# Experts ordered by token count on the chip, with 128, 64 or 32 slots each

## The chip, the cores and the metric

The kernel runs on one core of a Trainium2 chip. The metric is the device time of one launch in microseconds. Before the change three runs took 777.27, 777.66 and 778.37 us; the median is 777.66.

## The reference

One layer of a hybrid diffusion block on 256 context tokens and 256 latent tokens with 1024 channels, all in fp32:

```
mod  = SiLU(c) @ w_ada                      # shift, scale, gate; context and latent have their own c
h    = rms_norm(x) * (1 + scale) + shift
p    = h @ w_in                             # split among four mixers: SSD, GLA, RG-LRU, attention
x    = x + gate * (merge(mixers(p)) @ w_out)
h    = rms_norm(x) * (1 + scale2) + shift2  # latent tokens only from here
group  = top-1 of 4 groups; experts = top-2 of the 4 experts in that group; weights by softmax
out  = x + gate2 * sum over the two experts of  w * (silu(h @ w1[e]) * (h @ w3[e])) @ w2[e]
```

There are 16 experts with 512 inner channels; w1, w3 and w2 of one expert are 6 MB in fp32, so all experts together are 96 MB. Each latent token goes to two experts, 512 pairs in all.

## The kernel before, in words

**Front.** `ada` (L956 to L969) multiplies the two conditioning vectors with the modulation weights. The vectors stand in four columns of the array, two for the value rounded to fp32r and two for what the rounding leaves (`cs4`). A 1 MB load of weights comes as two halves; the even one is used in fp32 (L965), the odd one is split by ACT into a rounded part `whi` (L865) and by DVE into the rest `wlo` (L866), and both are multiplied (L968). `hk(k)` (L971 to L986) turns the sums of a channel block into columns (L975), transposes the normalized tokens (L979) and applies shift and scale.

**Middle.** The projection into the mixers, the mixers and the output projection run from L885 to L1812. The diff doesn't touch them.

**Routing.** The logits give one-hot marks `M` of the two experts of each token. A matmul with a triangle of ones counts, for each token and expert, the tokens ahead of it (`prv`), and a matmul of ones the tokens per expert. `val` (L388) is each token's slot in its expert, `cnt` (L393) the counts. `xh` and `xo` (L376) are the normalized tokens as rounded value and rest. `places` (L402 to L442) finds the first expert of 4 to 15 with over 64 tokens and exchanges it with position 11.

**Experts.** Each position has 64 slots, position 11 has 128 (`TWICE`). PE's order is written by hand. `one_hot` (L452) compares slots with a row of numbers and gives a matrix S of tokens by slots; `gather` (L481) multiplies tokens with S for four positions at once (256 columns), each of eight channel blocks with value and rest, and DVE scales the result (L487). `slot_weights` (L470) gives the routing weight of each slot. For an expert, `s1` (L506) computes w1 and w3 with 64 columns of the array each: w1 on the upper half HI, w3 on the lower half LO, 512 output columns each. `s1p` (L513, L514) does SiLU and product, `pick` (L521) transposes S, `s2` (L529) transposes the activations, `s3` (L542) multiplies with w2, two halves of the output on two halves of the array. ey, eyh and eyl (L549 to L551) scale with the gate and split into value and rest, `s4` (L557) scatters them with S back to tokens, adding into the two PSUM sums `eo0` and `eo1` over all experts. At the end eight additions (L658) and two transfers write the output.

Written order for each expert e: first half of s1(e+1), pick(e), s4(e-1), s2(e), second half of s1(e+1), s3(e). After every fourth expert the gather of the next four positions is spread around s3.

**Loads.** The 96 loads of 1 MB are issued by SP in the order of use into 15 buffers; a load waits until PE has read the buffer's former content. **Overflow.** At the very end a loop runs once per block of slots that no position had room for; with no such block it runs zero times.

Of the kernel before, what the change touches and what calls it, by code (L numbers as in the profile page):

```python
# [191 lines left out]
NE = 16  # L192
# [5 lines left out]
TWICE = 11  # L198
# [3 lines left out]
class Moe:  # L202


    def __init__(self, tc, I, xl, ident, identb, kp):
# [9 lines left out]
        self.identb = identb  # L215
        self.eps = kp.tile([128, 1], F32, name="eps2")
# [18 lines left out]
        self.ohu = kp.tile([128, NE], U8, name="ohu")  # L235
# [3 lines left out]
        self.val = kp.tile([128, 3, NE], F32, name="val")  # L239
        self.vp = kp.tile([128, 3, NE], F32, name="vp")  # L240
        self.Wp = kp.tile([128, 2, NE], F32, name="Wp")
        self.oh = kp.tile([128, NE], F32, name="oh")
        self.dif = kp.tile([128, 3, NE], F32, name="dif")
        self.ids = kp.tile([128, NE], mybir.dt.int32, name="ids")
        G.iota(self.val[:, 2], pattern=[[1, NE]], base=0, channel_multiplier=0, allow_small_or_imprecise_dtypes=True)
        self.prio = kp.tile([128, 2, NE], F32, name="prio")
        G.iota(self.prio[:, 0], pattern=[[-1, NE]], base=NE, channel_multiplier=0, allow_small_or_imprecise_dtypes=True)
        G.memset(self.prio[:, 0, 0:FIXED], 0.0)
        G.memset(self.prio[:, 1], 0.0)
        G.memset(self.prio[:, 1, TWICE:TWICE + 1], 0.5)  # L250
        self.cnt = kp.tile([128, NE], F32, name="cnt")
# [90 lines left out]
    def route(self, tp, tb):  # L342
# [22 lines left out]
        V.tensor_copy(self.ogt, self.og)  # L365
# [33 lines left out]
    def places(self):  # L399
# [3 lines left out]
        L, mg, og, le, ml, ex, rg = self.L, self.mg, self.og, self.le, self.ml, self.ex, self.rg  # L403
        M, W = self.M, self.W
        b4 = lambda ap: ap[:, :, None].to_broadcast([128, 2, 4])
        oh, m, ohu = self.oh, self.mo[:, 0:1], self.ohu
        vp, val = self.vp, self.val
        V.scalar_tensor_tensor(oh, self.cnt, float(CAP), self.prio[:, 0], op0=OP.is_gt, op1=OP.mult)
        V.tensor_tensor(oh, oh, self.prio[:, 1], op=OP.max)
        V.reduce_max(m, oh, axis=AX.X)  # L410
        V.tensor_copy(vp, val)
        V.tensor_scalar(ohu, oh, m, None, op0=OP.is_equal)
        P = slice(TWICE, TWICE + 1)
        V.copy_predicated(vp, ohu[:, None, :].to_broadcast([128, 3, NE]), val[:, :, P].to_broadcast([128, 3, NE]))
        V.tensor_scalar(oh, oh, m, None, op0=OP.is_equal)
        V.tensor_mul(self.dif, val, oh[:, None, :].to_broadcast([128, 3, NE]))
        V.reduce_sum(vp[:, :, P], self.dif, axis=AX.X)
# [20 lines left out]
        d = self.dif[:, 0:2]  # L438
        V.tensor_copy(self.Wp, self.W)
        V.copy_predicated(self.Wp, ohu[:, None, :].to_broadcast([128, 2, NE]), self.W[:, :, P].to_broadcast([128, 2, NE]))  # L440
        V.tensor_mul(d, self.W, oh[:, None, :].to_broadcast([128, 2, NE]))
        V.reduce_sum(self.Wp[:, :, P], d, axis=AX.X)  # L442

    def slots(self, g):

        self.S64 = self.kp.tile([128, 2, GE, CAP], F32R, name="S64", bufs=1)
        for t in range(2):
            i = self.one_hot(self.S64[:, t], (self.vp if g else self.val)[:, t, g * GE:g * GE + GE], GE)
        return i
# [6 lines left out]
    def run(self, out, mp, rp, ps, dump):  # L456
# [9 lines left out]
        def slot_weights(dst, n, Sx, Wx, c=CAP):  # L466
            p = tb()
            for i in range(n):
                for t in range(2):
                    T.matmul(p[0:c, i:i + 1], Sx(t, i).bitcast(F32), Wx(t, i), start=t == 0, stop=t == 1)  # L470
            V.tensor_copy(dst, p[0:c, 0:n])
# [18 lines left out]
        class Block:  # L490
            def __init__(self):
                self.wide, self.cs = False, [slice(0, 512)]
# [3 lines left out]
        def s1(b, half, post=True):  # L496
# [13 lines left out]
        def s1p(b):  # L510
            n = 2 * CAP if b.wide else CAP
            b.a = mp.tile([128, 512], F32, name="ef", bufs=2)[0:n]
            b.last = S.activation(b.a, b.p[0] if b.wide else b.p[0][HI], AF.Silu)  # L513
            b.last2 = V.scalar_tensor_tensor(b.a, b.a, b.w, b.p[1][0:n], op0=OP.mult, op1=OP.mult)  # L514

        def pick(b):
            n = 2 * CAP if b.wide else CAP
# [7 lines left out]
        def s2(b):  # L525
            n = 2 * CAP if b.wide else CAP
            ptv = tb()[:, 0:4 * n].rearrange("p (k s) -> p k s", k=4)
            for k in range(4):
                T.transpose(ptv[:, k], b.a[:, k * 128:k * 128 + 128], ident[0:n, 0:n])  # L529
            b.at = mp.tile([128, 4, 128], F32, name="eat", bufs=2)[:, :, 0:n]  # L530
            S.copy(b.at, ptv)

        def s3(b):
            n = 2 * CAP if b.wide else CAP
            p = (tb(), tb()) if b.wide else (tb(),) * 2
            for i in range(2):
                r = b.load(4 + i)
                for j in range(2):
                    k = 2 * i + j
                    for hf, pr in enumerate((slice(0, n), slice(0, n) if b.wide else HI)):  # L540
# [3 lines left out]
            for hf in range(2 if b.wide else 1):  # L544
# [3 lines left out]
                for s in b.cs:  # L548
                    V.tensor_mul(q[:, s], p[hf][:, s], self.gw[:, hf, s] if b.wide else self.gp[:, s])  # L549
# [4 lines left out]
        def s4(b):  # L554
            for s, i, t in [(s, i, t) for s in b.cs for i in range(2) for t in range(2)]:
                for hf, pr in enumerate((slice(0, 128),) * 2 if b.wide else (LO, HI)):
                    T.matmul(b.f[hf][:, t, s], b.st[pr, t], b.y[hf if b.wide else 0][i][pr, s],  # L557
                             start=b.start and i == 0, stop=b.stop and i == 1 and s is b.cs[-1])

        f = [ps.tile([128, 2, 512], F32, name=f"eo{hf}", bufs=1) for hf in range(2)]  # L560
        xgs = {}
        order = tc.manual_schedule(engines={mybir.EngineType.PE})
        order.__enter__()

# [5 lines left out]
        with tc.issue_after(group(0, at=4).ins):  # L570
            self.places()

        def expert(e):
# [7 lines left out]
            b.load, b.f, b.start, b.stop = load, f, e == 0, e == NE - 1  # L581
            if e == NE - 1:
                b.cs = [slice(0, 256), slice(256, 512)]
# [3 lines left out]
            b.x = lambda k: xgs[e // GE][:, k, (e % GE) * CAP:(e % GE) * CAP + CAP]  # L587
            b.Sb = lambda t: S64b[e // GE][:, t, e % GE]
# [14 lines left out]
        def weights(g):  # L603
            S64 = self.S64
            slot_weights(ws[:, g * GE:g * GE + GE], GE, lambda t, e: S64[:, t, e],
                         lambda t, e: Wp[:, t, g * GE + e:g * GE + e + 1])
            S64b[g] = kp.tile([128, 2, GE, CAP], BF, name="S64b", bufs=2)
# [10 lines left out]
        for hf, pr in enumerate((LO, HI)):  # L618
            V.tensor_copy(self.gp[pr], self.gw[pr, hf])
        for e in range(NE):  # L620
# [3 lines left out]
            if e % GE == GE - 2 and e < NE - GE:  # L624
                self.slots(e // GE + 1)
                weights(e // GE + 1)
# [7 lines left out]
            if e % GE == GE - 1:  # L634
# [19 lines left out]
        def add_out(f):  # L654
            for c, t in ((0, 0), (0, 1), (1, 0), (1, 1)):
                for hf in range(2):
                    s = slice(hf * 512 + c * 256, hf * 512 + c * 256 + 256)
                    V.tensor_add(xl[:, t, s], xl[:, t, s], f[hf][:, t, c * 256:c * 256 + 256])  # L658
# [1205 lines left out]
```

## Time and profile before

| | |
|---|---|
| median of three runs | 777.66 us |
| profiled execution: its own time | 779.12 us |
| span of that execution | 777.4 us |
| mean granted TensorE clock | 0.981 |
| PE busy | 747.6 us, 96% |
| DVE busy | 454.2 us, 58% |
| ACT busy | 394.4 us, 51% |
| bytes moved | 186.59 MB, mean 240 GB/s |

The profiled execution is one launch recorded by the hardware; its span runs from the first instruction to the last. A busy PE is not PE at its best rate: matmuls are pipelined and the records of neighbours overlap. The granted clock is a share of 2.4 GHz; 0.50 is 1.2 GHz.

### The profile page before, as it was taken

Reading aid. Unit: us, or ns where it says so; the run is one execution under the profiler, and the core shown is the slowest. Engines: PE = TensorE matmul, PEld = TensorE weight load, DVE = VectorE, ACT = ScalarE, POOL = GpSimd, SP = SyncE. Lnnn points to the kernel's source line nnn. Section 1 sums busy time; section 2 is a strip of 40 time slices with the busy share of each in tenths; the row PEclk is TensorE's granted clock in tenths of the full one; section 3 lists DMA queues with packets and bytes.
Section 4 is the critical chain, followed back from the end, with each engine's and each line's share of the span. In section 5 each row is a group of like instructions: output and inputs, shape, how many; then the busy total and the mean of one; then the engine's idle time right before and its main releaser. Section 6 shows DMA issues by size and latency. Waiting matters only on the chain.

```text
span 777.4 us, 10064 instructions
## 1 busy us (share of the span) xinstructions
PE 747.6 (96%) x3702; PEld 494.4 (64%) x3702; DVE 454.2 (58%) x875; ACT 394.4 (51%) x650; POOL 16.9 (2%) x74
## 2 busy tenths in 40 slices
PE   7999999997999999999999999998999999999994
PEld 3267787875888877767878788885444354444442
DVE  3576786986883699889687866645112122203223
ACT  6468669899945697566456544533212121212111
POOL 3000000000000000000000001000000000000000
PEclk9999999999899999999999999998999999999998
DMA  8764221223444255446645698738999999999921
GB/s 332 284 228 173 111 67 69 109 61 120 138 159 140 106 193 207 150 158 231 220 144 190 222 357 310 306 140 330 416 426 427 424 427 424 427 427 406 392 91 56
DMA packets 29043, 186.59 MB, mean 240 GB/s; under 512 B 3312, under 2 KB 3472, under 8 KB 9152
## 3 DMA queue, kind: packets, MB, share of 16 engines
q1 hardware_dynamic: 27760, 182.03, 60.4%
q0 software_dynamic: 1088, 3.37, 1.6%
q8 instruction: 30, 0.49, 0.2%
q10 hardware_dynamic: 144, 0.52, 0.2%
q14 instruction: 21, 0.17, 0.1%
HBM read 184.87 MB, written 1.05 MB: 239 GB/s over the span
## 4 chain that ended last, share of the span: by engine, by line
PE 77%; DVE 9%; ACT 7%; DMA 4%; issue 2%; SPq 0%; DVEq 0%; ACTq 0%
PE eh L506 16%; PE mm L885 12%; PE mm L886 11%; PE mm L887 11%; PE etp L542 8%; PE eo L557 2%; DMA lr<-in_adar_dram 2%; DMA xl<-in_x_dram 2%; DVE wlo L866 1%; ACT L785 1%; PE tp L1118 1%; PE mm L965 1%; PE eh L481 1%; ACT whi L865 1%; PE etp L481 1%
## 5 line engine op out<-in xcount | busy, mean ns | idle before, releaser
L865 ACT CAST whi<-raw 128x1024 fp32r<-128x1024 f32 x109 | 114.3, 1049 | 100.7 <-PE mm L887 70.6
L866 DVE TENSOR_TENSOR wlo<-raw,whi 128x1024 fp32r<-128x1024 f32 x109 | 132.7, 1219 | 55.1 <-ACT whi L865 54.2
L506 PE MATMUL eh<-eraw,xg 128*64 128x512 f32 x480 | 108.9, 596 | 0.3 <-DVE xg L487 0.3
L886 PE MATMUL mm<-wlo,hhi 128*128 128x512 f32 x240 | 98.6, 411 | 1.6 <-DVE wlo L866 1.6
L885 PE MATMUL mm<-whi,hhi 128*128 128x512 f32 x240 | 97.9, 411 | 0.0
L887 PE MATMUL mm<-whi,hlo 128*128 128x512 f32 x240 | 96.2, 402 | 0.0
L506 PEld LDWEIGHTS eh<-eraw,xg 128*64 128x64 f32 x480 | 34.6, 137 | 57.8 <-issue 52.6
L514 DVE SCALAR_TENSOR_TENSOR ef<-ef,wslot,eh 64x512 f32<-64x512 f32 x15 | 11.1, 739 | 99.1 <-ACT ef L513 99.1
L885 PE MATMUL mm<-hhi,whi 128*128 128x512 f32 (+1 forms) x168 | 67.0, 399 | 0.0
L886 PE MATMUL mm<-hlo,whi 128*128 128x512 f32 (+1 forms) x168 | 66.4, 395 | 0.0
L887 PE MATMUL mm<-hhi,wlo 128*128 128x512 f32 (+1 forms) x168 | 65.3, 389 | 0.0
L542 PE MATMUL etp<-eraw,eat 128*64 128x512 f32 (+1 forms) x256 | 61.4, 594 | 1.4 <-DVE xg L487 0.8
L885 PEld LDWEIGHTS mm<-whi,hhi 128*128 128x128 f32 x240 | 45.5, 190 | 13.0 <-issue 3.3
L886 PEld LDWEIGHTS mm<-wlo,hhi 128*128 128x128 f32 x240 | 45.7, 190 | 12.1 <-DVE wlo L866 1.9
L887 PEld LDWEIGHTS mm<-whi,hlo 128*128 128x128 f32 x240 | 45.6, 190 | 11.3 <-issue 1.1
L785 ACT ACT_TABLE_LOAD x39 | 50.0, 1283 | 0.8
L1085 DVE SCALAR_TENSOR_TENSOR lr<-lr,la 128x1024 f32<-128x1024 f32 x32 | 39.0, 1220 | 11.8 <-DMA lr<-in_adar_dram 11.6
L542 PEld LDWEIGHTS etp<-eraw,eat 128*64 128x64 f32 (+1 forms) x256 | 19.9, 140 | 38.2 <-issue 35.1
L513 ACT ACTIVATE ef<-eh 64x512 f32<-64x512 f32 (+1 forms) x16 | 9.5, 594 | 60.6 <-PE eh L506 60.6
L550 ACT CAST eyh<-ey 128x512 fp32r<-128x512 f32 (+1 forms) x18 | 10.6, 595 | 52.8 <-DVE ey L549 45.3
L887 PEld LDWEIGHTS mm<-hhi,wlo 128*128 128x128 f32 x168 | 31.6, 188 | 8.1 <-issue 1.5
L885 PEld LDWEIGHTS mm<-hhi,whi 128*128 128x128 f32 x168 | 31.6, 188 | 7.7 <-DVE lr L1085 0.8
(487 smaller groups left out, 1231.5 us busy)
## 6 DMA issues: line engine op xcount, KB each, us to landing
eraw<-in_ew_dram SPq DMA_DIRECT2D x96, 1024.0 KB, 12.4
raw<-in_ws_dram SPq DMA_DIRECT2D x59, 1024.0 KB, 4.8
lr<-in_adar_dram SPq DMA_DIRECT2D x32, 512.0 KB, 3.4
xc<-in_ctx_dram SPq DMA_DIRECT2D x1, 1024.0 KB, 7.1
xl<-in_x_dram SPq DMA_DIRECT2D x1, 1024.0 KB, 13.0
lw<-in_lw_dram POOLq DMA_DIRECT2D x4, 256.0 KB, 3.0
xl<-in_x_dram POOLq DMA_DIRECT2D x1, 1024.0 KB, 6.2
out_dram<-xl SPq DMA_DIRECT2D x1, 512.0 KB, 2.8
```

What stands on the lines that cost most here:

```text
L481: T.matmul(q, x[:, t, k * 128:k * 128 + 128], Sx(t), start=j == 0 and t == 0, stop=j == 1 and t == 1)
L506: T.matmul(b.p[m][pr], b.x(k), r[:, c:c + 512], start=k == 0, stop=k == 7)
L514: b.last2 = V.scalar_tensor_tensor(b.a, b.a, b.w, b.p[1][0:n], op0=OP.mult, op1=OP.mult)
L542: T.matmul(p[hf][pr], b.at[:, k], r[:, c:c + 512], start=k == 0, stop=k == 3)
L557: T.matmul(b.f[hf][:, t, s], b.st[pr, t], b.y[hf if b.wide else 0][i][pr, s], start=b.start and i == 0, stop=b.stop and i == 1 and s is b. ...
L785: S.activation(o, i, func, **kw)
L865: S.copy(hi, r)
L866: V.tensor_sub(lo, r, hi.bitcast(F32))
L885: T.matmul(ps, l[0], r[0], start=start, stop=False)
L886: T.matmul(ps, l[0], r[1], start=False, stop=False)
L887: lastmm[0] = T.matmul(ps, l[1], r[0], start=False, stop=stop)
L1085: V.scalar_tensor_tensor(r, r, 1.0, cb, op0=OP.mult, op1=OP.mult, accum_out=lcol[:, j, k:k + 1])
```

## The change

Experts 4 to 15 are ranked on the chip by their token counts, with 12 x 12 comparisons on DVE, and slots, identities and routing weights are moved to the ranked positions with products and sums (`move`). Position 9 gets the largest (128 slots), positions 4 to 8 the next five (64 slots), positions 10 to 15 the six smallest (32 slots, `FEW`). Experts 0 to 3 keep their positions. There are three gathers instead of four: positions 0 to 3, 4 to 7, and 8 with 10 to 15 (64 + 6 x 32 = 256 slots).

A position with 32 slots uses four quarters of the array's columns: w1 and w3 have two quarters each, with 256 output columns a quarter, and so has w2. Its s2 has two transposes instead of four, its scatter four row quarters of 256 columns. The sums `eo` are four PSUM tiles of 256 columns by two token blocks; they are zeroed once by matmuls with a zero matrix, and every scatter adds to them. A 64-slot scatter has 16 programs of 256 columns instead of 8 of 512. The last expert's predecessor has its scatter half before and half behind the last w2. Counts are copied by ACT right behind `val`. The overflow table has 15 entries of two numbers instead of 7.

In the front, `ada` uses all weights in fp32, without the split, as 32 programs on four column quarters (`cz` holds the two vectors and 30 zero columns; the quarters are summed afterwards by `pk`). Behind every four programs stand eight programs on the identity matrix whose result isn't used (`warm`). `hm` forms the modulation of four channel blocks at once.

The core of the diff:

```diff
-TWICE = 11
+TWICE = 9
+FEW, HALF = 10, 32
+GROUPS = [[(0, 4, CAP)], [(4, 4, CAP)], [(8, 1, CAP), (FEW, 6, HALF)]]
...
         V.scalar_tensor_tensor(self.val[:, 0:2], M, -1000.0, prv[:, 0:2], op0=OP.mult, op1=OP.add)
+        S.copy(self.cnt, prv[:, 2])
         self.last = i = self.slots(0)
         for t, h in ((1, 0), (0, 1), (1, 1)):
             i = low(t, h, i)
+        self.low = i
         with tc.issue_after(i.ins):
-            V.tensor_copy(self.cnt, prv[:, 2])
+            V.tensor_copy(self.ogt, self.og)
...
+        V.scalar_tensor_tensor(key, self.cnt[:, FIXED:NE], float(NE), self.kio, op0=OP.mult, op1=OP.add)
+        V.tensor_tensor(self.sq, row(key), down(key), op=OP.is_gt)
+        V.reduce_sum(rk, self.sq, axis=AX.X)
+        V.tensor_tensor(self.pm, row(rk), down(self.want), op=OP.is_equal)
+        def move(dst, src, n):
+            V.tensor_mul(self.dif[:, 0:n], src[:, :, None, FIXED:NE].to_broadcast([128, n, NS, NS]),
+                         self.pm[:, None].to_broadcast([128, n, NS, NS]))
+            V.reduce_sum(dst[:, :, FIXED:NE], self.dif[:, 0:n], axis=AX.X)
+            V.tensor_copy(dst[:, :, 0:FIXED], src[:, :, 0:FIXED])
...
+                    if b.few:
+                        for q in range(4):
+                            c = (2 * j + 1 - q // 2) * 512 + q % 2 * 256
+                            T.matmul(b.p[0][q * 32:q * 32 + 32, 0:256], b.x(k), r[:, c:c + 256], start=k == 0, stop=k == 7)
+                        continue
...
+                    if b.few:
+                        for q in range(4):
+                            T.matmul(p[0][q * 32:q * 32 + 32, 0:256], b.at[:, k % 2, k // 2 * 32:k // 2 * 32 + 32],
+                                     r[:, j * 1024 + q * 256:j * 1024 + q * 256 + 256], start=k == 0, stop=k == 3)
+                        continue
...
+                if b.few:
+                    for q in range(4):
+                        r = slice(q * 32, q * 32 + 32)
+                        T.matmul(b.f[q][:, t], b.st[r, t], b.y[0][i][r, 0:256], start=False, stop=b.stop and i == t == 1)
+                    continue
...
+            for p in f:
+                T.matmul(p.rearrange("p t (a b) -> p (t a) b", a=2), self.zero,
+                         identb[:, None, :].to_broadcast([128, 4, 128]), start=True, stop=False)
...
+                s4(B[e - 1], (0,))
                 s3(B[e])
-                s4(B[e - 1])
+                s4(B[e - 1], (1,))
                 s4(B[e])
...
-        NB, NF = 7, 3 * NE
+        NB, NJ = 15, 4
...
-            if len(w) == 1:
-                T.matmul(pm[0:4], cs4[:, kk].bitcast(F32), w[0][:, s], start=kk == 0, stop=kk == 7)
-                continue
-            for i in range(2):
-                T.matmul(pm[0:4], cs4[:, kk], w[i][:, s], start=kk == 0 and i == 0, stop=kk == 7 and i == 1)
-        S.copy(mr[c][:, a], pm[0:4])
+            o = (kk % 4) * 32
+            i = T.matmul(pm[o:o + 32], cz[:, kk], w[0][:, s], start=kk < 4, stop=kk >= 4)
+            if kk % 4 == 3:
+                warm(i)
+        S.copy(mr[c][:, a], pm)
+
+    def warm(after, n=8):
+        p = tpb()
+        with tc.issue_after(after.ins):
+            for _ in range(n):
+                T.matmul(p[:, 0:128], ident, ident, start=True, stop=True)
```

What stands in a row on PE at the start of the program, before (`raw` is a half used whole, `whi` and `wlo` are the split one):

```order
L931 MATMUL mm<-ident 128x128 x12
L965 MATMUL mm<-raw,cs_139 4x512 x2
L968 MATMUL mm<-whi,cs_139 4x512
L968 MATMUL mm<-wlo,cs_139 4x512
L968 MATMUL mm<-whi,cs_139 4x512
L968 MATMUL mm<-wlo,cs_139 4x512
L965 MATMUL mm<-raw,cs_139 4x512 x2
```

And of the change (L1036 is `ada`, L1045 `warm`, L1067 the transposes of normalized tokens, L1055 the modulation's sums):

```order
L999 MATMUL mm<-ident 128x128 x12
L1036 MATMUL mm<-raw,cz 32x512 x4
L1045 MATMUL tp<-ident 128x128 x8
L1036 MATMUL mm<-raw,cz 32x512 x4
L1045 MATMUL tp<-ident 128x128 x8
L1036 MATMUL mm<-raw,cz 32x512 x4
L1045 MATMUL tp<-ident 128x128 x8
L1067 MATMUL ac<-ident,xn 128x128 x4
L1036 MATMUL mm<-raw,cz 32x512 x4
L1045 MATMUL tp<-ident 128x128 x8
L1055 MATMUL tp<-pk,mr 128x2 x8
L1067 MATMUL ac<-ident,xn 128x128 x4
```

The programs on `whi` and `wlo` are gone, groups of eight on `ident` stand in between, and the first transposes stand behind the third group of four instead of among the sixth.

On DVE, from the first `xo` to the first scaled gather, before:

```order
L376 SCALAR_TENSOR_TENSOR xo<-xl,rs_4039,xh 128x512
L388 SCALAR_TENSOR_TENSOR val<-M,tp 128x32
L452 TENSOR_TENSOR S_4475<-val,iot 128x256 x2
L376 SCALAR_TENSOR_TENSOR xo<-xl,rs_4039,xh 128x512 x3
L393 COPY cnt<-tp 128x16
L411 COPY vp<-val 128x48
```

And of the change:

```order
L392 SCALAR_TENSOR_TENSOR xo<-xl,rs_4045,xh 128x512
L404 SCALAR_TENSOR_TENSOR val<-M,tp 128x32
L476 TENSOR_TENSOR S_4484<-val,iot 128x256 x2
L392 SCALAR_TENSOR_TENSOR xo<-xl,rs_4045,xh 128x512 x3
L411 COPY og<-o_4450 128x8
L432 SCALAR_TENSOR_TENSOR key<-val,kio 128x12
L441 COPY vp<-val 128x4x4
```

The copy of the counts is no longer on DVE behind the three `xo`; the ranking begins there instead.

On PE, the last expert and the scatter around it (L506 and L542 are w1/w3 and w2, L557 the scatter), before:

```order
L506 MATMUL eh<-eraw,xg 64x512 x8
L542 MATMUL etp<-eraw,eat 64x512 x8
L521 LDWEIGHTS S64b
L521 MATMUL etp<-identb,S64b 64x128
...
L529 MATMUL etp<-ident,ef 128x64 x4
L542 MATMUL etp<-eraw,eat 64x512 x8
L557 MATMUL eo_4497<-eyh,est 128x512
```

And of the change (L535, L576 and L599 are the same three):

```order
L535 MATMUL eh<-eraw,xg 32x256 x16
L576 MATMUL etp<-eraw,eat 32x256 x16
L555 LDWEIGHTS S64b
L555 MATMUL etp<-identb,S64b 32x128
...
L563 MATMUL eh<-ident,ef 128x64 x2
L599 MATMUL eo_4508<-eyh,est 128x256
...
L576 MATMUL etp<-eraw,eat 32x256 x16
L599 MATMUL eo_4508<-eyl,est 128x256
```

Programs of 64 columns and 512 outputs became twice as many of 32 columns and 256 outputs, and a half of the scatter of the expert before stands ahead of the last w2.

## Rows read from the trace of the kernel before

**Rows 1.** Windows by stage: length, PE, PEld, DVE, ACT, POOL busy (count), clock, DMA, GB/s.

```profile
0.00:43.40 43.40, 36.06 (x123) 13.24 (x123) 22.98 (x51) 25.17 (x42) 6.63 (x25) 0.92 0.83 302
43.40:516.00 472.60, 466.39 (x2243) 363.47 (x2243) 361.58 (x633) 316.06 (x506) 10.27 (x49) 0.99 0.48 171
516.00:535.40 19.40, 15.54 (x97) 13.53 (x96) 13.88 (x53) 6.43 (x12) 0.00 (x0) 0.82 0.78 321
535.40:742.80 207.40, 204.95 (x1104) 94.40 (x1106) 47.21 (x123) 42.22 (x83) 0.00 (x0) 0.99 0.99 411
742.80:768.60 25.80, 24.63 (x141) 9.76 (x136) 5.76 (x10) 4.53 (x10) 0.00 (x0) 1.00 0.01 2
768.60:777.40 8.80, 0.00 (x0) 0.00 (x0) 2.74 (x8) 0.00 (x0) 0.00 (x0) 0.64 0.31 123
```

**Rows 2.** Windows around the last landing, same columns.

```profile
741.00:743.00 2.00, 2.00 (x16) 1.00 (x14) 0.00 (x0) 0.37 (x1) 0.00 (x0) 1.00 0.79 332
743.00:745.00 2.00, 2.00 (x12) 0.72 (x10) 0.00 (x0) 0.00 (x0) 0.00 (x0) 1.00 0.05 20
```

**Rows 3.** Chain of waits, one 64-slot expert: start, us, engine, tile, line, count.

```profile
603.66 3.58 PE eh L506 x16
607.25 3.43 PE etp L542 x16
...
614.22 1.12 PE eo L557 x8
```

**Rows 4.** Chain of waits at the end.

```profile
760.80 0.70 DVE ey L549
...
766.12 2.51 PE eo L557 x24
768.62 0.41 DVE xl L658
```

**Rows 5.** Chain of waits in the routing.

```profile
526.86 1.99 DVE xo L376 x3
...
528.98 0.58 PE eh L481
```

**Rows 6.** Chain of waits in the front.

```profile
22.75 1.14 DVE wlo L866
...
43.46 0.66 PE mm L885 x2
...
47.36 0.44 PE ac L979 x4
```

**Rows 7.** Windows of L965 (one), then L968 (two): PE and PEld alone.

```profile
23.90:42.30 18.40, 10.50 (x20) 1.20 (x20) 0.92 0.80 286
...
23.90:42.30 18.40, 6.11 (x20) 1.43 (x21) 0.92 0.80 286
42.30:62.00 19.70, 0.85 (x4) 0.17 (x2) 1.00 0.57 200
```

**Rows 8.** Windows of L506: start of a 64-slot expert, then of the 128-slot one.

```profile
657.80:657.85 0.05, 0.05 (x2) 0.05 (x2) 1.00 1.93 819
...
692.40:692.45 0.05, 0.03 (x1) 0.03 (x1) 1.00 0.77 328
```

**Rows 9.** Chain of waits: weights, w1/w3 of the 128-slot expert, a gather's end.

```profile
542.53 0.88 PE etp L470 x16
...
692.49 7.06 PE eh L506 x16
...
713.72 0.94 PE eh L481 x8
714.66 0.94 PE etp L481 x8
```

**Rows 10.** Window of L340, 128x128 programs in the routing.

```profile
522.11:524.25 2.14, 2.14 (x11) 2.14 (x11) 0.50 1.02 425
```

**Rows 11.** L702, the table's accumulations: ns min/median/max, first and last start.

```profile
L702 DVE SCALAR_TENSOR_TENSOR osml<-osml x14: 195/207/211, 736.2 to 740.4; 128x48 f32<-128x48 f32 x14
```

More of the change, by code (lines that the diff above doesn't have):

```diff
@@ L197 @@
 GE = 4
-TWICE = 11
+TWICE = 9
+FEW, HALF = 10, 32
+GROUPS = [[(0, 4, CAP)], [(4, 4, CAP)], [(8, 1, CAP), (FEW, 6, HALF)]]
+PLACE = {}
+for _g, _parts in enumerate(GROUPS):
+    _o = 0
+    for _p, _n, _c in _parts:
+        for _i in range(_n):
+            PLACE[_p + _i] = (_g, _o, _c)
+            _o += _c
 NBUF = dict(raw=8, more=7)
@@ new lines, in places @@
+        vp, val, key, rk, NS = self.vp, self.val, self.key, self.rk, NE - FIXED
+        n2 = NS * NS
+        x2 = x2.rearrange("p a b -> p (a b)")
+        v2 = lambda a: a.rearrange("p (a b) -> p a b", a=NS)
+        self.sq, self.pm = v2(x2[:, 0:n2]), v2(x2[:, n2:2 * n2])
+        self.dif = x2[:, 2 * n2:6 * n2].rearrange("p (j a b) -> p j a b", j=4, a=NS)
+        row = lambda ap: ap[:, None, :].to_broadcast([128, NS, NS])
+        down = lambda ap: ap[:, :, None].to_broadcast([128, NS, NS])
@@ L418, in places @@
+        move(vp, val, 4)
         V.tensor_copy(self.ids, self.vp[:, 2])
@@ L569, in group, with part @@
             return gather(lambda k: xgs[g][:, k], lambda t: S64[:, t], GE, ks, at)
-        with tc.issue_after(group(0, at=4).ins):
-            self.places()
+        def part(a, e):
+            o, c = PLACE[e][1:]
+            return a[:, o:o + c]
+        group(0, at=4)
+        with tc.issue_after(self.low.ins):
+            self.places(mp.tile([128, 8, 128], F32, name="x2", bufs=1))
         def expert(e):
@@ L580, in load @@
                 return r
-            b.load, b.f, b.start, b.stop = load, f, e == 0, e == NE - 1
-            if e == NE - 1:
-                b.cs = [slice(0, 256), slice(256, 512)]
+            b.load, b.f, b.stop = load, f, e == NE - 1
+            b.late = e in (TWICE, TWICE - 1)
+            if e >= FEW:
+                b.few, b.cs = True, [slice(0, 256)]
             if e == TWICE:
@@ L623, in run @@
                     wide(B[TWICE])
-            if e % GE == GE - 2 and e < NE - GE:
-                self.slots(e // GE + 1)
-                weights(e // GE + 1)
+            if e in (2, 6):
+                self.slots(e // 4 + 1)
+                weights(e // 4 + 1)
             if e == NE - 1:
@@ L678, in small @@
             return r
-        fl = small([128, 3, NE], F32, name="ofl")
-        oh1 = small([128, NE], F32, name="oh1")
-        for j in range(3):
-            V.tensor_scalar(fl[:, j], cnt, float(CAP * (j + 1)), None, op0=OP.is_gt)
-        V.tensor_mul(oh1, fl[:, 0], self.oh)
-        V.tensor_sub(fl[:, 0], fl[:, 0], oh1)
+        fl = small([128, NJ, NE], F32, name="ofl")
+        bio = small([128, NJ, NE], F32, name="obio")
+        for j in range(NJ):
+            V.tensor_scalar(bio[:, j], self.cap, float(CAP * j), None, op0=OP.add)
+        V.tensor_tensor(fl, vp[:, 3:4].to_broadcast([128, NJ, NE]), bio, op=OP.is_gt)
         flv = fl.rearrange("p j e -> p (j e)")
@@ L726, in run @@
             gather(lambda k: xo_[:, k, 0:CAP], lambda t: So[:, t, 0], 1)
-            fo = [ps.tile([128, 2, 512], F32, name=f"eo{hf}", bufs=1) for hf in range(2)]
+            fo = sums()
             b = Block()
@@ L859, in prep @@
         r = raw_half(i)
-        if spec[i][0] == "ada" and i % 2 == 0:
+        if spec[i][0] == "ada":
             prepped[i] = (r,)
+            if i % 2 == 1:
+                raw_load()
             return
@@ new lines, in hk @@
+    def hk(ks):
+        for k in ks:
+            md, j = mds[k // 4], k % 4
+            pt = acb()
+            for i in range(4):
+                T.transpose(pt[:, i * 128:i * 128 + 128], xn[:, i, k * 128:k * 128 + 128], ident)
+            h = st.tile([128, 512], F32, name="h", bufs=2)
+            V.tensor_scalar(h[:, CTX], pt[:, CTX], md[:, j, 0, 0:1], md[:, j, 1, 0:1], op0=OP.mult, op1=OP.add)
+            act(h[:, LAT], pt[:, LAT], AF.Identity, scale=md[:, j, 0, 1:2], bias=md[:, j, 1, 1:2])
+            S.copy(hid[:, k], h)
+            V.tensor_sub(lod[:, k], h, hid[:, k].bitcast(F32))
@@ L987, in body @@
     ada(0, 0)
     ada(0, 1)
+    hm(0)
+    hk((0, 1))
     ada(1, 0)
-    for k in range(4):
-        hk(k)
+    hk((2, 3))
     ada(1, 1)
-    for k in range(4, 8):
-        hk(k)
+    hm(1)
+    hk(range(4, 8))
     identb = cp.tile([128, 128], BF, name="identb")
```

185 lines of the change are left out of this document (96 added, 89 removed).

## The prediction

> **What bounds the kernel now.** I read first where the time lies by stage, then where the last weights land, then one expert in the chain of waits, then the two places at which the change touches that chain outside the experts. The stages [rows 1]: up to 43.4 the modulation (`ada`), to 516 the mixers, to 535.4 the routing, to 742.8 the experts while weights arrive, to 768.6 experts without arrivals, then adds and the output. The reader is to see the DMA column: 0.99 for 207.4 us, then 0.01 while PE is busy for 24.63 of 25.80. The last of the 96 expert loads lands at about 742.8 [rows 2], where the DMA share falls from 0.79 to 0.05. So PE ends 25.8 us behind the weights, and the end is PE's.
>
> Per expert PE is nonetheless the quicker one. In the chain a 64-slot expert is 16 records of w1/w3 (3.58), the same again, 16 of w2 (3.43), and a scatter of 1.12 [rows 3], with transposes between about 11.9 us. The 81 loads that are not prefetched take 207.4 us [rows 1], 2.56 each with the start-up in it, 15.4 per expert. The lag of 25.8 us is the 15 prefetched loads (38 us) not yet worked off, since the extras (gathers, the 128-slot expert) cost PE what the single experts win. Therefore: whatever is taken off PE anywhere among the experts moves the end one for one, until 25.8 us are gone; after that only arrivals count.
>
> At the end the chain runs through ey (0.70), eyh, the last w2 and 24 scatter records from 766.12 on (2.51) [rows 4], and 8.8 us of adds and output follow [rows 1]. In the routing, PE's first gather starts at 528.98, right behind `cnt`, which stands on DVE behind three `xo` of 1.99 us [rows 5]. In the front, PE runs from 23.94 almost without a gap; before it stands `wlo`, 1.14 us on DVE, and the first projection follows at 43.46 [rows 6], and the two forms of `ada` fill 10.50 and 6.11 of its 18.40 us [rows 7].
>
> **The change: experts.** The router's counts, worked out from the reference on its inputs, are for experts 4 to 15, sorted: 70, 47, 37, 36, 33, 31, 27, 27, 25, 21, 21, 13. So 128, five times 64 and six times 32 slots hold everything; no overflow block runs.
>
> The large term is quarters. A program of before computes 512 columns for 64 slots on half of the array; two of them write the two halves. Of the pair the trace shows that both are under way within the first 0.05 us (2 records at 657.80; a 128-slot expert, which has the whole array, has 1) [rows 8], and 16 records of a half expert take 3.58 us, while 16 of the 128-slot expert take 7.06 [rows 9]. So halves run beside each other. No row shows four quarters beside each other. Bounds: if four run as two do, w1/w3 costs half of 7.16, w2 half of 3.43; if only two at a time, nothing is gained; if they run singly, it doubles. I take the first, as the nearest row is the pair at full overlap. For six experts: w1/w3 6 x 3.6 = 21.5, w2 6 x 1.7 = 10.3. The scatter of an expert has half the columns in quarters: 6 x about 0.5 = 3. One gather of four is gone (0.94 + 0.94 and its first half, taken as the same: 2 x 1.9 = 3.8) [rows 9]; with its waits I put it at 4.5. The weights of slots grow by 24 programs in quarters at 0.055 (16 records in 0.88) [rows 9]: +1.3. Together PE loses 38 us, more than its lag of 25.8.
>
> So PE will wait for arrivals in the last experts, and the end is: last landing 742.8, plus 0.7 (middle of 0 to 1.4, for loads that wait for a buffer around the wide expert, which comes two places earlier, when PE is still further behind), plus what is behind the landing. That is half of w2 in quarters (0.9), ey on 256 columns (0.4, from 0.41 for an add of 256 [rows 4]), eyh about as much, and the scatter, whose 24 records took 2.51: 1.6, as part of it now stands before the last w2. With waits 3.3, so PE ends at 746.8 instead of 768.6. As PE will wait for more than half of the last experts, part of the tail can stand at the lower of the two clocks, as a stretch of the routing does at 0.50 (1.2 GHz) [rows 10]: +1. **Experts: -20.7** (from -23.5 with everything short to -18 with waits). The ranking on DVE and the table of 30 small accumulations instead of 14 stand in a stage in which DVE is busy 47.21 of 207.40 us [rows 1]; they hide behind arrivals. Without this cover the 16 added ones at 0.21 [rows 11] would cost 3.4 us, once.
>
> The Trainium skill ("TensorE: Matmul & The Clock Gate", Part 3, "Packing small matmuls — row/col tiling") says that matmuls begin and end strictly in program order, and only weight loads are pulled ahead. An fp32 program is two passes here; by that rule only the last pass of one quarter could lie over the first of the next, and four quarters would take as long as two halves. The first records of the pair [rows 8] speak against it, since the second program's record begins before the first one's second pass. By the rule experts would come to -4 instead of -20.7; it is the first rival. The same section gives a measured speed-up of 3.07 for four row tiles and 2.38 for three column tiles; no run here shows either, and by 3.07 a quad would cost 0.65 of a pair, PE would lose 29 us among the experts instead of 38, and the sum would stay.
>
> **Routing.** ACT now copies the counts behind `val`, and the PSUM bank that PE's gather needs is no longer held over the three `xo`. The gather can go 1.99 us sooner, less the copy: -1.8 (bounds 0, if `hi` copies or the half clock take over, and -2.2). The first buffer is released that much sooner, so the arrivals move with it. The longer placing on DVE lies beside the first experts' work, before whose `ef` it has to be done: `wslot` is needed after 7 us of w1/w3. Zeroing the sums is four programs in PE's idle time.
>
> **Front.** `ada` loses its low halves: from 22.75 on PE is rid of 10.50 + 6.11 + 0.85 (behind 42.3) and the start loses `wlo` 1.14 [rows 6, 7]: -18.6. Five of eight quads stand behind `xn`, each two passes of 0.43 if quarters overlap: +4.4. Five groups of eight warming programs follow, sixteen passes each; four passes of this size take 0.44 at full clock [rows 6], 11 records touch 2.14 us at half [rows 10], so 1.8 a group, 3.3 at half: +9.0, and one group at half +1.5. The three modulation steps in one on DVE put 1 us between: +1. **Front: -2.7** (-18.6 + 4.4 + 9.0 + 1.5 + 1). Bounds, from there: four more groups at half clock +6, quads two at a time +4.4, both +8 in the end; one by one +13. Below, -8 if most of the warming falls into waits.
>
> The mixers (43.4 to 516) are the same instructions in the same order, so they only shift.
>
> **Sum.** 779.1 of the profiled run (777.4 of span and 1.7 around it) - 2.7 - 1.8 - 20.7 = 753.9. The profiled run stands 1.5 above the median of 777.66, so 752.4.
>
> **Rivals.**
> 1. Quarters don't beat halves (in order, or two at a time). For it: each program is still a pass pair, and no row has four. Against: the pair's starts. Then experts -4 (gather, weights, scatter), routing -1.8, front -2.7 + 4.4 = +1.7: -4 in all, or about 0 with the warming at half clock: 774 to 778.
> 2. Quarters gain in part, say 0.85 of the halves' time. For it: nothing that the rows exclude. Against: the pair, which loses nothing. PE is then rid of 0.15 x 63.5 (six times 7.16 + 3.43), 4.5 of gather and 1 of scatter, less 1.3: 13.7, under its lag, so that all of it counts: -18 in all, 760; with the warming at half clock 766.
> 3. Slower: an overflow block. If the seventh of experts 4 to 15 had over 32 tokens, the loop at the end would load a whole expert with nothing to hide it: six loads at 2.56 (15.4), last w2, ey, scatter, adds and output again (1.7 + 1.4 + 1.1 + 8.8): 28 us at least. From the first block: 752.4 + 28 = 781 or above. The counts say 27, five below the limit; a tie or a changed input would be needed. The serial quarters, at +60, would end here too.
>
> **Chances.** Forecast 0.72, its own range 746 to 762. Rival 1 0.13, of which a third lies within 0.2% and the rest on both sides, mostly faster. Rival 2 0.09. Rival 3 with serial quarters 0.06. About 0.2% (1.6 us) is what a measurement can tell from no change. Faster 0.88, same 0.05, slower 0.07. The range: the forecast's own, up to 768 for the partial gain, down to 744 if front and tail come out short.
>
> **What would show it.** Right: in the few experts' w1/w3, four records start within 0.05 us and 16 programs of a half take about 1.8 us; PE waits for arrivals in experts 12 to 15; last landing at 738 to 740; PE's end 3 to 5 us behind it. Routing: the first gather starts right behind `xo` or over it. Front: the first projection at about 41. Wrong: groups of two at a time and w1/w3 at 3.6 per half (rival 1); PE without a gap to the end (rival 2); a second pass through the loop's loads behind the adds (rival 3); warming groups of 3.4 us each would take the front's gain.

## The result, and the profile after

The changed kernel takes 756.11 us (median of 4 runs, 753.66 to 757.86) against 777.46 of the kernel before in the same set of runs; the ratio is 0.9723, 95% interval 0.9697 to 0.9749. Forecast were 752.4, with 744 to 768 as the range. The profiled execution has a span of 754.6 us against 777.4.

The same stages as in [rows 1], windows of the changed kernel (length, PE, PEld, DVE, ACT, POOL busy with counts, clock, DMA share, GB/s):

```profile
0.00:45.00 45.00, 38.16 (x281) 28.54 (x282) 14.95 (x46) 20.07 (x39) 6.90 (x26) 0.96 0.85 311
45.00:513.80 468.80, 461.52 (x2213) 359.64 (x2212) 358.04 (x622) 312.76 (x500) 10.31 (x51) 0.99 0.48 171
513.80:530.30 16.50, 13.22 (x102) 11.36 (x100) 13.87 (x47) 8.10 (x15) 0.00 (x0) 1.00 0.74 298
530.30:738.60 208.30, 195.65 (x1586) 97.30 (x1586) 50.54 (x163) 38.29 (x83) 0.00 (x0) 0.96 1.00 415
738.60:745.30 6.70, 5.90 (x64) 2.91 (x64) 1.33 (x4) 0.76 (x3) 0.00 (x0) 0.64 0.04 18
745.30:754.60 9.30, 0.00 (x0) 0.00 (x0) 2.69 (x8) 0.00 (x0) 0.00 (x0) 0.58 0.30 116
```

The stretch in which PE works with hardly any arrivals was 25.80 us and is 6.70. The stretch with arrivals has kept its length (207.40 and 208.30): it is the same 96 loads at about the same rate (411 and 415 GB/s). The routing has gone from 19.40 to 16.50, and PE's clock in it from 0.82 to 1.00. The last stretch of work stands at a clock of 0.64.

The chain of waits over the last experts of the changed kernel (start, us, engine, tile, line, count; L535 is w1/w3 in quarters, L576 w2 in quarters, L599 the scatter in quarters), the counterpart of [rows 3, 4]:

```profile
692.21 1.86 PE eh L535 x32
694.07 1.73 PE etp L576 x32
695.80 0.93 PE eh L535 x17
696.72 19.39 DMA eraw<-in_ew_dram
...
716.23 19.59 DMA eraw<-in_ew_dram
...
735.86 1.94 PE etp L576 x16
737.80 0.23 PE etp L555 x8
...
738.11 0.37 ACT est L557
738.48 0.31 ACT eyh L590
...
738.84 0.80 PE eo L599 x6
739.64 3.62 PE etp L576 x32
...
743.28 0.44 DVE ey L588
...
743.79 0.41 ACT eyh L590
...
744.25 1.01 PE eo L599 x15
```

Half of a small expert's w1/w3 takes 1.86 us where a 64-slot expert takes 3.58, its w2 1.73 where that takes 3.43. From 696.72 to 735.82 the chain is transfers: PE has caught up, and waits for a load of the experts for the first time until 708.94. From 735.86 on it is PE, ACT and DVE again: the last two loads aren't in it, because PE, at the lower clock, still has earlier work left when they land (the last of their packets ends at 740.30). The 32 records of w2 that took 1.73 us at 694 take 3.62 at 739.64.

That four quarters run side by side is seen where they start. Windows of L535 of the changed kernel (PE, PEld, clock, DMA, GB/s), the counterpart of [rows 8]:

```profile
692.20:692.25 0.05, 0.05 (x4) 0.05 (x8) 1.00 2.32 983
```

Four records are under way at once, where a pair was in [rows 8]: by the trace they begin within 0.02 us at 692.14, the next four at 692.38 and four more at 692.59.

**Where the 22.7 us of the two profiled spans come from**, by points that both have: the projection's matmul that has 40 recorded ones ahead of it, called the 40th here (57.39 before, 54.09 after), the last but one of the same lines, called the last (515.81, 513.77; it belongs to the output projection, and the stretch between the two is called the mixers), the first w1/w3 of an expert (535.44, 530.33), PE's end (768.58, 745.22), the end of the span (777.37, 754.63). The front gives -3.3, the mixers take +1.3 back, the routing gives -3.1, the experts -18.2, the output takes +0.6.

### The profile page after: what moved, and what is told of

Read it like the earlier page. It is cut to its first block, busy times and chain, and to the rows that moved or that the text cites. A ratio compares the mean times of both kernels' runs of the same rounds, so it can differ in the third digit from the quotient of the medians.

```text
span 754.6 us, 11136 instructions
## 1 busy us (share of the span) xinstructions
PE 714.4 (95%) x4242; PEld 499.7 (66%) x4242; DVE 441.4 (58%) x885; ACT 380.0 (50%) x637; POOL 17.2 (2%) x77
## 4 chain that ended last, share of the span: by engine, by line
PE 75%; DMA 11%; DVE 6%; ACT 6%; issue 1%; SPq 0%; DVEq 0%; ACTq 0%
PE mm L953 13%; PE mm L955 13%; PE mm L954 13%; PE eh L539 11%; DMA eraw<-in_ew_dram 5%; PE etp L581 5%; DMA lr<-in_adar_dram 4%; DMA xl<-in_x_dram 2%; PE eo L603 2%; ACT L851 2%; PE tp L1205 1%; PE tp L1045 1%; PE eh L535 1%; PE etp L576 1%; DVE lr L1172 1%
## 5 line engine op out<-in xcount | busy, mean ns | idle before, releaser
L933 ACT CAST whi<-raw 128x1024 fp32r<-128x1024 f32 x101 | 106.0, 1050 | 92.2 <-PE mm L955 65.9
L934 DVE TENSOR_TENSOR wlo<-raw,whi 128x1024 fp32r<-128x1024 f32 x101 | 123.2, 1222 | 48.3 <-ACT whi L933 47.8
L539 PE MATMUL eh<-eraw,xg 128*64 128x512 f32 x288 | 65.4, 597 | 0.3 <-DVE xg L514 0.3
L548 DVE SCALAR_TENSOR_TENSOR ef<-ef,wslot,eh 64x512 f32<-64x512 f32 (+1 forms) x15 | 9.5, 633 | 79.7 <-ACT ef L547 79.7
L539 PEld LDWEIGHTS eh<-eraw,xg 128*64 128x64 f32 x288 | 20.4, 137 | 33.9 <-issue 31.1
L581 PE MATMUL etp<-eraw,eat 128*64 128x512 f32 (+1 forms) x160 | 39.7, 595 | 0.3 <-DVE xg L514 0.3
L954 PEld LDWEIGHTS mm<-hlo,whi 128*128 128x128 f32 x168 | 31.6, 188 | 7.4 <-issue 1.4
L547 ACT ACTIVATE ef<-eh 64x512 f32<-64x512 f32 (+2 forms) x16 | 8.2, 514 | 52.1 <-PE eh L539 39.1
```

The costliest lines, as they stand in the source:

```text
L548: b.last2 = V.scalar_tensor_tensor(b.a, b.a, b.w, b.p[1][0:n, cs], op0=OP.mult, op1=OP.mult)
L581: T.matmul(p[hf][pr], b.at[:, k], r[:, c:c + 512], start=k == 0, stop=k == 3)
L933: S.copy(hi, r)
L934: V.tensor_sub(lo, r, hi.bitcast(F32))
L954: T.matmul(ps, l[0], r[1], start=False, stop=False)
```

## The experiments

**The same kernel again.**

> The changed kernel itself, run beside the others as their base. Its earlier runs lie between 753.66 and 757.86 us. If the spread comes from one `lr` load of the attention stage that lands late in some executions (in the profiled one PE loses 1.5 us there at 331 us), this profile will show that stretch with another loss, and all else within 0.3 us of the first profile. Expected 754 to 758.

755.83 us (753.77 to 757.57), ratio 0.9721 (0.9701 to 0.9742). As expected the stretch at 331 us has no loss here, but another one does: the 40th projection program stands at 53.76, the last at 513.23, with 1.7 us lost near 445 us, behind another `lr` load. The routing also differs: 18.16 us from the last projection program to the first w1/w3, not 16.56, with PE at 0.50 from 524 to 526. So the second half of the expectation (all else within 0.3 us) was wrong: two executions of one kernel differ by 1.6 us in the routing, in where they lose 1.5 to 1.7 in the mixers, and in the tail. The spread of 4 us over the runs has room for these; the unprofiled runs don't show which of them fell where.

**Quarters undone.**

> Quarters undone: the six small positions keep 32 slots, the places, the gathers and the loads, but w1, w3 and w2 are computed as two programs of 512 columns on two column groups of 32 instead of four programs of 256 on four. Theory A (four quarters run side by side, PE catches up with the arrivals, and that is where the gain comes from): w1/w3 of a small expert goes back from 3.72 to 7.16 us and w2 from 1.73 to 3.43, 31 us in all on PE; about 6.5 us of that is spare (PE ends 6.7 us behind the last landing now), and most of the rest moves the end: 770 to 776 us. Theory B (the gain comes from the ranked places, the dropped gather and the routing; quarters don't beat halves): 755 to 758, as now.

```diff
-                        for q in range(4):
-                            c = (2 * j + 1 - q // 2) * 512 + q % 2 * 256
-                            T.matmul(b.p[0][q * 32:q * 32 + 32, 0:256], b.x(k), r[:, c:c + 256], start=k == 0, stop=k == 7)
+                        for m, pr in enumerate(PR[::-1]):
+                            c = (2 * j + m) * 512
+                            T.matmul(b.p[0][pr], b.x(k), r[:, c:c + 512], start=k == 0, stop=k == 7)
```

(`PR` is columns 0 to 31 and columns 64 to 95; w2 and the scatter are changed alike.) 773.39 us (771.28 to 776.79), ratio 0.9957 (0.9938 to 0.9977): theory A. The chain of waits of this kernel (L536 w1/w3, L577 w2):

```profile
736.54 3.43 PE etp L577 x16
739.97 2.22 PE eh L536 x11
...
743.52 1.15 PE eo L597 x16
744.88 3.56 PE eh L536 x16
748.44 2.22 PE etp L577 x11
```

Each half costs what it cost before. From the first w1/w3 to PE's end it takes 232.0 us, against 213.3 and 214.9 in the two profiles with quarters and 233.1 before. Quarters are worth 17 to 19 us; all else that the change does among the experts is worth only 1.1 net. The kernel also shows what the overflow table on DVE costs where PE is the bound: ey at 727.42 stands behind fourteen of its thirty accumulations, which begin at 723.79, and PE is idle for 1.35 us (windows of this kernel):

```profile
727.50:731.20 3.70, 2.35 (x26) 1.55 (x22) 3.49 (x13) 1.60 (x3) 0.00 (x0) 1.00 1.01 423
```

**One expert less.**

> Position 15 is left out, its six loads and its work (its tokens' contributions are missing in the output). Theory A (the last experts wait for arrivals): six loads less are 6 x 2.46 = 14.7 us, with the same tail: 740 to 743. Theory B (PE's work sets the end): only that expert's PE work goes, 3.72 + 1.73 + about 1.2 of transposes and scatter = 6.7 us: 748 to 750.

```diff
-        self.order = order
+        self.order = [x for x in order if x[0] < NE - 1]
-        for e in range(NE):
+        for e in range(NE - 1):
```

739.75 us (738.77 to 741.47), 16.1 less than the kernel run again and just under theory A's range. From the first w1/w3 to PE's end it takes 198.9 us, 14.5 and 16.0 less than in the two profiles of the changed kernel, where six loads at 2.46 make 14.8. The 6.7 us of PE's work that theory B has are far from it. So the end is set by arrivals, to within what two profiles of one kernel differ by.

**The old front.**

> The new routing and experts behind the old front (`ada` with the split weights, no warming groups). If the new front is worth what the projection's 40th program shows (3.3 us earlier) and 1.5 of it is given back later in the mixers, as in the profile: 757.5 to 760. If the front's gain is lost altogether by the time of the routing: 755 to 757.

The core of the edit (the vectors, the splitting of the weights and the order of the front's steps are put back too):

```diff
-            o = (kk % 4) * 32
-            i = T.matmul(pm[o:o + 32], cz[:, kk], w[0][:, s], start=kk < 4, stop=kk >= 4)
-            if kk % 4 == 3:
-                warm(i)
+            for i in range(2):
+                T.matmul(pm[0:4], cs4[:, kk], w[i][:, s], start=kk == 0 and i == 0, stop=kk == 7 and i == 1)
```

757.39 us (756.40 to 760.77), ratio 0.9759 (0.9734 to 0.9784); 1.6 more than the kernel run again, though the intervals touch. The profile is clearer: the 40th projection program stands at 57.80, 3.7 and 4.0 later than in the two profiles with the new front. At the end of the mixers the distance to the two profiles with the new front is 2.3 and 2.9, so in these two a part of what the front gains is given back; to the profiles of the runs with halves and with counts on DVE, which have the new front too, it is 4.1 and 3.7, and nothing is given back. The median lies just under the first range of the expectation; that the gain is lost altogether the profile doesn't bear out. By time alone the front's worth is not shown.

**No warming programs.**

> The new front without its warming groups (64 programs on the identity matrix left out). Theory A (they are pure cost: five groups of 1.98 us stand on PE's path behind the normalization): up to 9.9 us less, if neither arrivals nor the clock take it; the ten MB ahead of the projection can't land before about 28 us, so PE can be done with `ada` by then: 747 to 751. Theory B (they hold the clock at 2.4 GHz): without them PE waits for arrivals and runs `ada`, the transposes and the first projections at 0.50, about 1 us more for each of five quads, 2 for the transposes, 2 for the sums, and several for the projection: 754 to 760.

753.97 us (751.67 to 755.04), ratio 0.9701 (0.9682 to 0.9720). By time it isn't told apart from the kernel run again (the intervals overlap). The median lies between the two theories' ranges, and its profile has both effects. Windows of this kernel:

```profile
20.00:25.00 5.00, 4.15 (x20) 1.65 (x17) 2.78 (x5) 0.59 (x1) 0.00 (x0) 0.50 0.90 354
...
35.00:40.00 5.00, 2.60 (x23) 1.79 (x16) 1.36 (x5) 1.35 (x3) 0.00 (x0) 0.91 1.02 413
40.00:45.00 5.00, 4.96 (x15) 3.53 (x16) 4.02 (x5) 4.23 (x6) 0.00 (x0) 0.50 0.46 157
```

PE runs at 0.50 from 20 to 25 us, and again from 40 to 45, behind five microseconds in which it is busy for only 2.60. The 40th projection program comes at 53.24, only 0.5 to 0.9 earlier, though 10 us of programs are gone from PE's path. The rest of the 1.9 us between the medians is not in the front.

**Three warming programs instead of eight.**

> Three programs instead of eight in each warming group of the front. With none the kernel took 753.97 us, with eight 755.8; with none PE ran at 0.50 from 20 to 25 and from 40 to 45 us. Theory A (five of eight programs are pure cost and three keep the clock): 5 groups x 5 programs x 0.25 us = 6 us less on PE's path, of which DVE and ACT steps of the modulation take half: 751 to 753.5. Theory B (three don't keep the clock, or arrivals and ACT set the front's end): 753.5 to 755.5.

753.06 us (749.47 to 760.69), ratio 0.9700 (0.9658 to 0.9741), a spread of 11 us. Its profile has the 40th projection program at 51.43, the earliest of all. The kernel that also has another order at the end (below) has it at 52.40, and the one with the tail's waits filled too at 58.21, with the same front. Windows of the last one:

```profile
25.00:30.00 5.00, 5.00 (x25) 5.00 (x25) 0.37 (x3) 0.41 (x1) 0.00 (x0) 0.50 0.66 220
```

and of the one at 52.40:

```profile
25.00:30.00 5.00, 5.00 (x44) 3.70 (x48) 2.15 (x7) 2.05 (x4) 0.00 (x0) 1.00 0.81 244
```

With three programs the front stood at either clock in different executions, and the two differ by 6 us. With eight it stood at 1.00 from 20 to 50 us in all seven profiles of kernels that have them, with the 40th projection program at 53.6 to 54.1. So the eight go with a steady clock; three are faster when the clock holds. Theory A for the profile; the median lies in its range too, but the interval overlaps that of the kernel run again.

**Counts copied on DVE.**

> The counts are copied by DVE behind the three `xo` again, all else as in the changed kernel. Theory A (the routing's gain is the gather that need not wait for the three `xo`): the first gather starts 1.9 us later, and so does everything behind it, arrivals included: 1.5 to 3 us more than the changed kernel's 755.9, so 757.3 to 759; the upper end if PE falls to 0.50 in the gather as in the kernel before. Theory B (the gain is the clock's alone, or another wait is behind the copy): within 0.7 of 755.9.

```diff
-        S.copy(self.cnt, prv[:, 2])
         with tc.issue_after(i.ins):
+            V.tensor_copy(self.cnt, prv[:, 2])
```

757.18 us (754.23 to 758.24), ratio 0.9740 (0.9715 to 0.9766). By time it isn't told apart from the kernel run again. From the last projection program to the first w1/w3 it takes 19.09 us; in the twelve profiles of kernels whose counts ACT copies it is 16.54 to 18.48. PE's clock is 1.00 throughout this stretch; in the three of the twelve of which that is true too (one of them the changed kernel's first profile) it takes 16.54 to 16.56, 2.5 us less. That speaks for theory A, with a cause of delay that I had not named: the chain of waits of this kernel shows the ranking on DVE ahead of the gather's scaling.

```profile
523.39 1.99 DVE xo L392 x3
525.38 0.09 DVE val L410
...
526.94 0.72 DVE x L438
...
527.81 0.66 DVE vp L440
528.47 0.90 DVE xg L514 x2
```

**Waits of the last experts filled.**

> In positions 13 to 15 four programs that add zeros to the sums stand behind the work of every load but the last two, 0.22 us each; PE's waits there are filled with them. Theory A (the tail of the changed kernel is PE at 0.50: 3.62 us for 32 records of w2 that take 1.73 at full clock, and 1.94 before it): tail shorter by up to 3.5 us where an execution fell to 0.50 there, by nothing where it didn't; median 753 to 755. Theory B (the arrivals alone set the end, or the added programs delay the work of the next load): 755.5 to 757.5.

```diff
+        def dummy(b):
+            for _ in range(4 if b.busy else 0):
+                T.matmul(b.f[0].rearrange("p t (a b) -> p (t a) b", a=2), self.zero,
+                         identb[:, None, :].to_broadcast([128, 4, 128]), start=False, stop=False)
```

756.41 us (751.73 to 758.01), ratio 0.9718 (0.9689 to 0.9748): no gain in the median. The profile shows that the aim was reached (this kernel):

```profile
735.00:740.00 5.00, 5.00 (x58) 1.88 (x51) 0.62 (x2) 0.38 (x1) 0.00 (x0) 1.00 0.91 374
```

against 0.50 in the same window of the changed kernel:

```profile
735.00:740.00 5.00, 4.10 (x42) 1.94 (x42) 0.85 (x2) 0.84 (x3) 0.00 (x0) 0.50 0.67 274
```

From the first w1/w3 to PE's end it is 211.5 us, 1.8 to 3.4 less than in the two profiles of the changed kernel; but of the two other profiles with filled waits (the combinations below) one has 213.3 and one 216.4. That filling shortens this stretch is therefore not shown. The chain of waits of this kernel has the added programs (L620) in it, beside w1/w3 of one load (L535): in this profile PE is the bound again in place of arrivals, as theory B has it.

```profile
703.53 0.97 PE eo L620 x4
704.50 1.00 PE eh L535 x16
705.50 0.97 PE eo L620 x4
```

This execution also lost 5.3 us in the mixers, where the two of the changed kernel lost 1.1 and 1.3.

**Three combinations and the price of a block.**

> Three warming programs a group in the front, the zero-adding programs behind the loads of positions 13 to 15, and the last expert's w2 ahead of the whole scatter of the expert before. If the front's 2 us (three programs, 753.06) and the tail's (from the first s1 to PE's end 211.5 us in the profile with filled waits, 213.3 to 214.9 without) add up, and the order takes 0.5 more: 750 to 752.5. If the mixers give the front's part back, or the filled waits only delay the last loads' work: 753 to 756.

> As the run before it, but without the zero-adding programs. If filling the waits is worth 1.5 to 3 us, this one is that much slower: 752 to 754.5, and its profile shows w2 of the last expert at 0.50 in some executions. If filling is worth nothing: the same as the run before it within 1 us.

> As the first of these with no warming programs in the front at all. With none the front's first projections ran at 0.50, and yet the kernel was 1.9 us faster than with eight. If three are better than none by the 0.9 us that the medians gave: 751 to 753.5, above the first of these; if both are within the spread: the same within 1 us.

```diff
-                s4(B[e - 1], (0,))
                 s3(B[e])
-                s4(B[e - 1], (1,))
+                s4(B[e - 1])
```

755.05 us (753.68 to 761.62, ratio 0.9733, 0.9712 to 0.9754), 755.22 (751.05 to 755.66, ratio 0.9716, 0.9693 to 0.9739) and 757.67 (752.85 to 758.64, ratio 0.9754, 0.9728 to 0.9781). None is shown to beat the changed kernel; the parts don't add up. The first lies in the upper range of its expectation, the second within 0.2 of the first (filling is worth nothing), the third 2.6 above the first, which neither branch of its expectation has. In the first one's profile the experts take 216.4 us, the most of all with quarters, and PE is busy without a gap at full clock from 730 to 745. The added programs stand in its chain of waits as above, which fits theory B of the run with filled waits.

> The limit of the six small positions in the overflow table is set to 26 instead of 32, so that the two experts with 27 tokens get a block each (one token each, added twice in the output). Prices one turn of the loop, the third rival of the prediction: at 28 us or more a block (six loads of 2.56, then w2, scatter, adds and output with nothing beside them) it takes 812 us or more; if the loads of the second block run beside the first, 795 to 805.

```diff
-        G.memset(self.cap[:, FEW:NE], float(HALF))
+        G.memset(self.cap[:, FEW:NE], 26.0)
```

814.94 us (2 runs), 59.1 more than the kernel run again for two blocks, 29.6 each. The forecast's 28 or more holds, but not by its terms: in the second turn's chain of waits the arrivals don't appear.

```profile
781.25 0.56 PE etp L497 x4
781.81 1.84 PE eh L508 x8
...
789.22 3.08 PE eh L539 x8
...
792.42 5.18 PE eh L539 x24
...
800.02 3.68 PE etp L581 x16
...
805.17 1.40 PE eo L603 x13
```

The turn is placing, gather, w1/w3, w2 and scatter one behind the other on PE, which stands at 0.50 from 780 to 790, and its loads lie beside them.

## Why the prediction was right, and where its terms were off

The mechanism among the experts was right at each of its main steps. PE was the bound, 25.8 us behind the arrivals; four quarters start together and halve w1/w3 and w2; PE then catches up and the end is set by arrivals (undoing the quarters gives 17 to 19 us back, leaving out six loads takes 16.1). What I drew from the rule of the Trainium skill ("TensorE: Matmul & The Clock Gate", Part 3, "Packing small matmuls — row/col tiling"), that quarters would be no faster than halves, doesn't happen: the trace has four records under way at once and 32 in 1.86 us. What fails is my inference from two passes, not the rule itself: the records begin one after the other, about 7 ns apart. Whether that is the program's order the trace doesn't tell. Next to nothing is lost from two groups to four (1.86 of 3.58 and 1.73 of 3.43, 1.92 and 1.98 times as fast), which is more than the 1.53 that I estimate from the same section's 3.07 for four row tiles, over a pair that loses nothing; these are column tiles.

The sum was 3.7 us too low (752.4 against 756.1). Of that the terms make 2.5 (-25.2 forecast, -22.7 between the first profiles). The other 1.2 is the step from profile to median: the profiled execution of before stood 1.5 above its median, that of the changed kernel 0.2 above its own. By terms, from the two profiles of the changed kernel:

- **Front, -2.7:** -3.3 and -3.6 at the 40th projection program. That it comes near the forecast is partly luck. The terms were added up for the first projection program, forecast at about 41; it begins at 42.89 and 42.56, only 0.5 and 0.8 earlier than before. The other 2.8 us arise behind it: the modulation's sums and transposes, which before stand between projection programs until 55.05, are through at 45.31. Chain of waits of the changed kernel (L1055 the sums, L1067 the transposes), then of the one before (L979 the transposes):

```profile
25.57 1.68 PE tp L1055 x16
...
40.74 1.70 PE tp L1055 x16
...
44.20 1.11 PE ac L1067 x8
```

```profile
55.05 0.44 PE ac L979 x4
```

 The forecast had no term for the sums. Groups of warming cost 1.98 us at full clock, not 1.8; the quads 1.00, not 0.87; no group behind `xn` stood at half clock, for which 1.5 was put aside.
- **Mixers, 0:** +1.3 and +1.1. This step failed as a fixed zero. The instructions are the same and in the same order, but they don't merely shift: an `lr` load that lands later against the program's work makes DVE and then PE wait. The chain of waits in the changed kernel:

```profile
325.63 5.42 DMA lr<-in_adar_dram
...
331.08 1.23 DVE lr L1172 x2
...
333.10 1.13 PE tp L1731 x2
```

 That is where the first profile loses 1.5 us; the second loses its part elsewhere. It is no fixed price of the change either: in the five other profiles with this front the mixers take from 0.4 us less to 5.3 more than in the one profile of before. Why the landings differ was not tried.
- **Routing, -1.8:** -3.1 and -1.5. The wait behind the three `xo` is gone; what differs is the clock, 1.00 throughout in one and 0.50 for 2 us in the other.
- **Experts, -20.7:** -18.2 and -19.8 (the forecast's own figures, 746.8 + 1 against 768.6, give -20.8). The term mis-sized is the tail. I had the last landing 208.1 us behind the first w1/w3 and PE's end 4.3 behind the landing. By the packets in the traces the last load ends 210.0 us behind the first w1/w3 in the first profile (740.30) and 209.8 in the second (741.17), 1.9 and 1.7 later than I had it; before it was 208.2. In the first PE ends 4.9 us later, because it stands at 0.50 until 742, where 1 us was put aside for that: w2 alone takes 1.9 more. In the second the clock recovers. Windows of the second:

```profile
734.00:736.00 2.00, 1.72 (x16) 0.68 (x16) 0.40 (x1) 0.00 (x0) 0.00 (x0) 0.50 1.01 418
736.00:738.00 2.00, 1.54 (x20) 0.64 (x20) 0.00 (x0) 0.00 (x0) 0.00 (x0) 0.50 0.64 258
738.00:740.00 2.00, 1.44 (x26) 0.80 (x18) 0.79 (x2) 0.84 (x3) 0.00 (x0) 0.82 0.17 70
740.00:741.60 1.60, 1.16 (x24) 0.42 (x16) 0.06 (x1) 0.00 (x0) 0.00 (x0) 1.00 0.04 15
```

 The DMA share glides from 1.01 to 0.04 over 6 us, where before it fell from 0.79 to 0.05 between two windows of 2 [rows 2]; the chain's last transfer ends at 741.60. Behind it stand w2 1.11, ey 0.44, eyh 0.41 and the scatter 1.01, 3.1 with the gaps, as forecast (3.3).
- **Output, 0:** +0.6 (9.4 instead of 8.8), not forecast.

Of the rivals, the first fell with the quarters undone, the second with the times of w1/w3, the third is priced right and doesn't occur with these counts.

## What to carry to other kernels

When an engine is the bound only because it lags behind arrivals, a saving is worth its full size up to that lag and nothing beyond; read the lag off the window in which transfers stop. Behind that point the price of the tail is the last landing and a short chain at whatever clock the waiting engine has left, so size both from rows at the low clock too. And a saving early in a program has to be followed to the end, over several executions: here 3.3 us at 54 us were 2.0 at 514 in one, and in others nothing was lost or more than all of it.

## What the runs showed of the hardware that was not expected

Four column groups of 32 lose next to nothing against two of 64: 32 records of 256 columns on quarters took 1.86 us, 16 of 512 on halves 3.58.

Where PE waited for arrivals its clock went up and down between 0.50 and 1.00, differently in two executions of one kernel (0.50 from 734 to 742 in one; 0.50 from 734 to 738 and 1.00 from 740 on in the other). In the profile with filled waits it stood at 1.00 from 700 to 745.

When the reader waits for them, the last loads don't end together: the mean share of the DMA engines fell over 6 us, not over 2. By the packets of the second profile, some 16 are under way at a time until 736, five at 738, and from 739.25 to 741.17 a single one, 8 KB every 0.31 us, as of one engine that is behind the others (the trace doesn't name it); before, 16 are until 742.25 and none from 743.75. Why was not tried.
